# Padding few-row operands and grouping narrow column tiles on TensorE in a two-layer hybrid decoder step

## Chip, cores and metric

The kernel runs on one core of a Trainium2 chip. The metric is the device time of one execution in microseconds (us). The engines are named as the profile names them: PE (TensorE matmuls), PEld (TensorE weight loads), DVE (VectorE), ACT (ScalarE), POOL (GpSimd) and SP (SyncE, which issues most DMAs).

## What is computed

One inference step of a decoder with two layers, on a prompt of 512 tokens and on 8 samples of 4 new tokens each (T = 544 tokens in all, which share every weight). Cut to what matters:

```python
def hybrid_layer(x, conv_hist, S0, mem_k, mem_v, pos, lb, attend, lw):
    hn = rmsnorm(x, norm_g)
    z = hn @ w_in
    (c_h, c_b, c_c, hg_q, hg_f, hg_i, q_lat, kv_lat, k_pe, m_q, sg, mg) = jnp.split(z, offs, axis=-1)
    y_conv = c_b * conv
    o_hg, S = hgrn2_chunked(hg_q * HG_DK ** -0.5, kk, hg_i, logf, S0)
    y_hg = rmsnorm(o_hg, hg_g)
    q = rmsnorm(concat(q_nope, rope(q_pe, pos)), gq)
    c = rmsnorm(kv_lat, kv_norm_g)
    o_lat = attend(q, c, rope(k_pe, pos), w_uk, gk)
    y_mla = o_lat @ w_uv
    y_mem = softmax(rmsnorm(m_q, mem_gq) @ mem_k.T * MEM_SCALE) @ mem_v
    ys = stack([y_conv, y_hg, y_mla, y_mem]) * silu(sg)
    merged = sum(sigmoid(mg) * (ys @ w_bout))
    return x + merged @ w_o, new_hist, S, c, r
```

The prompt attends to itself (MLA) and to a memory of 256 rows. Each sample attends to its own cached latents (2048 past tokens, held in pages), to its own memory keys and values, and has its own HGRN state. All data are float32.

## The kernel before

Activations are held feature-major: 128 features on the partitions, 544 tokens in the columns. The bulk of the work is a list of items (`items`, filled from line 1385 on), each one weight tile of w_in, w_branch_out, w_out or the memory projections. A bulk weight and its operand are each split into a high and a low part of type float32r (`wh`, `wl`; `Hh`, `Hl` and the like), and each product is made of three matmuls of 128 rows, 128 columns and 272 moving columns (half of the tokens), into the PSUM tile `big`. The driver loop loads the next weights (`load`, line 1471), splits them on ACT and DVE (`conv`, line 1478), issues an item's first half, one step of lane A, the second half, the evacuation, and one step of lane B.

The lanes are Python generators that do the rest in plain float32, into the PSUM tile `sm`. A plain float32 matmul stands in the trace as two matmul instructions ("halves" below), a transpose as one.

- Lane A (`lane_a`, line 703): memory attention. For each of 8 samples `s_s` (line 767) makes the scores, four matmuls whose outputs take 32 rows of PSUM each, one per head; `s_t` transposes, `s_v` (line 788) multiplies by the values, eight matmuls of 32 output rows. `load_b` (line 756) loads keys and values of the next sample. Then `hgrn` (line 833), once per head: products inside blocks (`a_mm`), products between blocks of 64 and of 32 tokens, which write 64 and 32 rows of PSUM, the samples' keys and values made token by token in three groups of 32 rows, transposes of values and keys (line 964), and `psy`, eight matmuls of 32 output rows with the samples' states `s0`.
- Lane B (`lane_b`, line 1020): latent attention. `q_mm` (line 1090) multiplies by a weight of 192 rows in two parts, 128 and 64 rows; `k_sum` (line 1074) sums squares of four heads, each into 32 rows; `k_norm` (line 1084) spreads a norm from one row of a group of 32. The samples' softmax over the cached latents is cut into `soft1` to `soft5` (lines 1287 to 1338); `soft2` transposes 16 columns, `soft3` multiplies 16 rows by ones, `soft4` multiplies 17 blocks of probabilities by the latents, the last of them the new tokens (`cnew`, 32 rows).

How many rows an operand has, and how many rows of PSUM its output takes, sets the tiling of the array that a matmul is built with: 128x128, 128x64, 128x32, 64x128, 32x128 or 32x32 (rows x columns). In the built program before, the tiling changes 408 times from one matmul to the next.

The order on each engine is not written by hand. A scheduler with a timeline of its own takes the instructions in the order of the Python code as priorities and moves each to where it expects its operands; on the chip each engine then runs its instructions strictly in that order.

All matmuls go through the helper `mm` (line 169), so that in the trace nearly all are line 170; ACT is line 173, `tensor_tensor` line 179. The lines that the steps below speak of, as they stand:

```python
                mm(ps[64 * hf:64 * hf + 32, 256 + c * 32:256 + (c + 1) * 32], X[32][:, q:q + 32], X[32][:, q + 32:q + 64])
...
            mm(ps[:, 0:16], ones[0:16], g["m"][0:16, 32:48])
...
                mm(ps[:, 0:HT], wuqB[0:64, h * P:(h + 1) * P], qB[0:64, c], start=False)
```

Of the kernel before, what the change touches and what calls it, by code (L numbers as in the profile page):

```python
# [46 lines left out]
def _z_tiles():  # L47
    """Column tiles of w_in: key -> 128 column numbers."""
# [27 lines left out]
# packed gain columns  # L76
# [8 lines left out]
# packed constant columns  # L85
# [51 lines left out]
def hybrid_kernel(ctx: ExitStack, tc: tile.TileContext, a, o):  # L137
# [9 lines left out]
    sp = pool("sp", 10)  # L147
# [21 lines left out]
    def mm(out, lhsT, rhs, start=True, stop=True):  # L169
        TE.matmul(out, lhsT, rhs, start=start, stop=stop)  # L170
# [49 lines left out]
    cnew = kp.tile([TS, P], F32, name="cnew")  # L220
# [11 lines left out]
    row4 = kp.tile([P, P], F32R, name="row4")  # L232
    csq = kp.tile([P, T], F32, name="csq")

    def setup_first():
        V.memset(ones, 1.0)
        V.memset(epsc, EPS)
        x = t("b")[:, 0:P]
        G.memset(x, 0.0)
        for r in range(0, P, 32):  # L240
            G.memset(x[r:r + 1, :], 1.0)
        V.tensor_copy(row4, x)
        S.dma_start(out=gn, in_=a["gains"])

    def scale_rows(s1, s2):
        """The row numbers of the cached latents, by four tokens."""
# [50 lines left out]
    def rstd_small(ss, n, alloc=None, eng=None):  # L297
        """The same for a narrow [rows, w]: a first guess from the exponent, then three Newton steps."""
# [35 lines left out]
    # ------------------------------------------------------------ driver state  # L334
# [17 lines left out]
    # ------------------------------------------------------------ bulk matmuls  # L352
# [60 lines left out]
    # ------------------------------------------------------------ norms of x and memory  # L413
# [55 lines left out]
    def mem_rstd(ms):  # L469
        """1/rms of every memory token, as a column."""  # L470
# [14 lines left out]
    # ------------------------------------------------------------ evacuations  # L485
# [51 lines left out]
    def ev_B(l):  # L537
        def run(it):
            lane[0] = "b"
            qB, rt, tmp = t(), t(), t()  # L540
            act(v2(qB[0:64]), ps2(it)[0:64], AF.Copy)
# [6 lines left out]
            act(sqB[0:64], qB[0:64], AF.Square)  # L548
# [153 lines left out]
    # ------------------------------------------------------------ lane A: memory attention, then HGRN  # L702
    def lane_a(l):
# [52 lines left out]
        def load_b(b):  # L756
            ks, vs = [], []
            for g in range(2):
                k = t()
                SY.dma_start(out=k[:, 0:512], in_=a["mkT"][l, b, :, g * 512:(g + 1) * 512])  # L760
                ks.append(k)
                v = t()
                SY.dma_start(out=v[:, 0:512], in_=a["mv"][l, b, :, g, :])
                vs.append(v)
            kvb[b] = (ks, vs)

        def s_s(b):
            ps = sm()
            for h in range(4):
                mm(ps[32 * h:32 * h + 32, 0:256], mqn[h][:, TP:T], kvb[b][0][h // 2][:, (h % 2) * 256:(h % 2 + 1) * 256])  # L770
# [17 lines left out]
        def s_v(b, pt):  # L788
            ps = sm()
            for j in range(2):  # L790
                for h in range(4):
                    mm(ps[32 * h:32 * h + 32, 0:P], pt[:, 256 + j * P + 32 * h:256 + j * P + 32 * h + 32],
                       kvb[b][1][j][:, h * P:(h + 1) * P], start=(j == 0), stop=(j == 1))
# [5 lines left out]
            del kvb[b]  # L799

        pp, pt_ = {}, {}
        for u in range(6):
            if u == 5:
                load_b(0)
# [28 lines left out]
    def hgrn(l, h):  # L833
# [38 lines left out]
            # one Newton step makes the two exact reciprocals  # L872
# [41 lines left out]
        mm(pss[0:32, 0:32], K4[:, TP:T], Q4[:, TP:T])  # L914
        put(2, ps)
        V.copy_predicated(AT[0:32, TP:T], m8[0:32, 0, 0:32], pss[0:32, 0:32])
# [6 lines left out]
        # factors that leave the chunk  # L923
# [23 lines left out]
        for hf in range(2):  # L947
# [690 lines left out]
```

## Time and profile before

| | |
|---|---|
| median of 3 runs | 1776.54 us (1776.44 to 1778.98) |
| profiled execution, span from first to last instruction | 1777.1 us |
| PE busy | 1751.2 us, 99% of the span, 14058 matmul instructions |
| PEld busy | 1647.5 us, 93% |
| DVE, ACT, POOL busy | 1083.0, 852.2 and 321.7 us (61%, 48%, 18%) |
| DMA | 201.12 MB, mean 113 GB/s |
| TensorE clock granted over the span | 0.997 |

The page gives no other time of the profiled execution than its span. A busy time counts overlapping matmuls once; matmuls are pipelined, so a busy PE may still be losing time between two starts. The page's strip of the span in 40 slices shows PE at nine tenths or more in every slice but the first. The other views used are the timeline (instructions in the order of their starts, equal ones merged), the list of waits, and a table of busy times by stretch.

### The profile page before, as it was taken

Reading aid. Unit: us, or ns where it says so; the run is one execution under the profiler, and the core shown is the slowest. Engines: PE = TensorE matmul, PEld = TensorE weight load, DVE = VectorE, ACT = ScalarE, POOL = GpSimd, SP = SyncE. Lnnn points to the kernel's source line nnn. Section 1 sums busy time; section 2 is a strip of 40 time slices with the busy share of each in tenths; the row PEclk is TensorE's granted clock in tenths of the full one; section 3 lists DMA queues with packets and bytes.
Section 4 is the critical chain, followed back from the end, with each engine's and each line's share of the span. In section 5 each row is a group of like instructions: output and inputs, shape, how many; then the busy total and the mean of one; then the engine's idle time right before and its main releaser. Section 6 shows DMA issues by size and latency. Waiting matters only on the chain.

```text
span 1777.1 us, 36029 instructions
## 1 busy us (share of the span) xinstructions
PE 1751.2 (99%) x14058; PEld 1647.5 (93%) x14058; DVE 1083.0 (61%) x2468; ACT 852.2 (48%) x1651; POOL 321.7 (18%) x327
## 2 busy tenths in 40 slices
PE   7999999999999999999999999999999999999999
PEld 5888889999999999999988798899999999999999
DVE  6666554658787886342464655456788878743332
ACT  5646334655656573222346554355557565622231
POOL 4010001012233432101130100001122343221110
PEclk9999999999999999999999999999999999999999
DMA  6312441233425343223453124423333343232233
GB/s 226 115 60 75 144 144 66 91 119 122 137 87 159 103 149 100 90 78 100 157 166 103 52 95 144 132 65 105 121 123 121 109 143 127 90 105 92 76 115 119
DMA packets 106828, 201.12 MB, mean 113 GB/s; under 512 B 13921, under 2 KB 48098, under 8 KB 106658
## 3 DMA queue, kind: packets, MB, share of 16 engines
q1 hardware_dynamic: 99346, 177.79, 31.5%
q0 software_dynamic: 7168, 20.98, 3.7%
q8 instruction: 111, 1.82, 0.4%
q14 instruction: 59, 0.48, 0.1%
q10 hardware_dynamic: 144, 0.04, 0.0%
HBM read 186.72 MB, written 12.04 MB: 112 GB/s over the span
## 4 chain that ended last, share of the span: by engine, by line
PE 91%; ACT 3%; DVE 3%; issue 2%; POOL 1%; DMA 1%; SPq 0%; ACTq 0%; DVEq 0%
PE big L170 68%; PE sm L170 21%; ACT ta L173 1%; DVE wl L179 1%; ACT wh L173 1%; ACT L173 1%; DVE e L176 1%; PE sm L964 0%; PE sm L739 0%; ACT tb L173 0%; PE sm L1187 0%; DVE Ml L179 0%; PE sm L1268 0%; DMA ta<-in_memT 0%; DVE Hl L179 0%
## 5 line engine op out<-in xcount | busy, mean ns | idle before, releaser
L170 PE MATMUL big<-Hh,wh 128*128 128x272 f32 x2528 | 741.9, 294 | 1.1 <-ACT Hh L173 0.6
L170 PE MATMUL big<-Hh,wl 128*128 128x272 f32 x2528 | 738.4, 292 | 2.8 <-DVE wl L179 2.7
L170 PE MATMUL big<-Hl,wh 128*128 128x272 f32 x2528 | 735.0, 291 | 2.0 <-DVE Hl L179 1.5
L170 PEld LDWEIGHTS big<-Hh,wh 128*128 128x128 f32 x2528 | 477.2, 189 | 12.2 <-issue 7.4
L170 PEld LDWEIGHTS big<-Hh,wl 128*128 128x128 f32 x2528 | 476.2, 188 | 12.1 <-issue 6.3
L170 PEld LDWEIGHTS big<-Hl,wh 128*128 128x128 f32 x2528 | 476.8, 189 | 9.2 <-issue 5.0
L173 ACT ACTIVATE wh<-wr 128x1024 fp32r<-128x1024 f32 (+1 forms) x246 | 232.9, 947 | 465.8 <-PE big L170 384.0
L179 DVE TENSOR_TENSOR wl<-wr,wh 128x1024 fp32r<-128x1024 f32 (+1 forms) x246 | 276.2, 1123 | 262.0 <-ACT wh L173 261.6
L173 ACT ACTIVATE tb<-sm 128x256 f32<-128x256 f32 (+6 forms) x380 | 141.1, 400 | 112.2 <-PE sm L170 84.6
L179 POOL TENSOR_TENSOR M<-M,e 128x544 f32<-128x544 f32 x48 | 87.7, 1827 | 403.5 <-DVE e L176 368.3
L170 PE MATMUL big<-ysh,wl 128*128 128x272 f32 x512 | 149.3, 292 | 0.0
L170 PE MATMUL big<-ysl,wh 128*128 128x272 f32 x512 | 148.4, 290 | 0.0
L170 PE MATMUL big<-ysh,wh 128*128 128x272 f32 x512 | 148.3, 290 | 0.0
L170 PE MATMUL sm<-ta 128*128 128x128 f32 (+5 forms) x1360 | 142.8, 284 | 0.0
L170 PEld LDWEIGHTS sm<-ta 128*128 128x128 f32 (+2 forms) x1360 | 106.6, 148 | 21.3 <-issue 9.6
L173 ACT ACTIVATE ta<-ta 128x544 f32<-128x544 f32 (+3 forms) x180 | 95.5, 538 | 52.4 <-DVE ta L179 38.9
L179 DVE TENSOR_TENSOR ta<-ta 128x256 f32<-128x256 f32 (+3 forms) x248 | 111.1, 481 | 10.1 <-ACT ta L173 9.3
L170 PE MATMUL sm<-Rh,rb 128*128 128x272 f32 x512 | 105.0, 294 | 0.0
L1206 POOL DMA_INDIRECT tb<-in_lat,row4i x64 | 72.0, 1125 | 180.2 <-PE sm L170 65.9
L1206 POOL DMA_INDIRECT tb<-in_rop,row4i x64 | 73.0, 1141 | 171.6 <-PE sm L170 56.2
L188 DVE TENSOR_REDUCE s<-tb 128x8 f32<-128x512 f32 (+1 forms) x150 | 99.8, 671 | 5.1 <-issue 4.6
L170 PEld LDWEIGHTS big<-ysh,wh 128*128 128x128 f32 x512 | 96.4, 188 | 0.7 <-issue 0.4
(233 smaller groups left out, 2551.2 us busy)
## 6 DMA issues: line engine op xcount, KB each, us to landing
wr<-in_w_in SPq DMA_DIRECT2D x158, 512.0 KB
wr<-in_wb SPq DMA_DIRECT2D x64, 256.0 KB
tb<-in_latT SPq DMA_DIRECT2D x256, 64.0 KB
ta<-in_mkT SPq DMA_DIRECT2D x32, 256.0 KB
ta<-in_mv SPq DMA_DIRECT2D x32, 256.0 KB
wr<-in_wo SPq DMA_DIRECT2D x16, 512.0 KB
ta<-in_shg SPq DMA_DIRECT2D x16, 256.0 KB
out_hgs<-ta SPq DMA_DIRECT2D x16, 256.0 KB
```

Source lines behind the costliest of these rows:

```text
L170: TE.matmul(out, lhsT, rhs, start=start, stop=stop)
L173: S.activation(out, in_, f, **k)
L176: V.scalar_tensor_tensor(out=out, in0=in0, scalar=sc, in1=in1, op0=op0, op1=op1)
L179: (eng or V).tensor_tensor(out=out, in0=in0, in1=in1, op=op)
L188: V.tensor_reduce(out=out, in_=in_, op=op, axis=AX.X, **k)
L1206: G.indirect_dma_start(out=out, out_offset=None, in_=a[src], in_offset=bass.IndirectOffsetOnAxis(ap=idx, axis=0))
```

## The change

Operands of few rows get the full 128 rows, with zeros below (`qB`, `wuqB`, `wukT` to 96 rows, `cnew`, `row4`, the small softmax tile `m`, the samples' HGRN products), so that their matmuls have the tiling 128x128 or stay in the one around them. Products of narrow outputs that stood apart are put together: `issue_after(first)` queues what is traced in its block behind the matmul `first` on PE. The HGRN products between blocks of 64 tokens are made in two halves of 32 rows. The samples' keys and values in HGRN are copied four times side by side by POOL and transposed as full tiles, where six matmuls made them. Memory keys are loaded two samples ahead and values two steps ahead of their use. In the built program the tiling changes 118 times. Zeros are written by POOL. The count of weight tiles and of bulk matmuls stays.

```diff
-    sp = pool("sp", 10)
+    sp = pool("sp", 8)
+    mp = pool("mp", 2)
...
-    row4 = kp.tile([P, P], F32R, name="row4")
+    row4 = kp.tile([P, 4, P], F32R, name="row4")
...
+            G.memset(qB[64:128], 0.0)
...
         for u in range(10):
+            first = s_v(u - 2, ss.pop(u - 2)) if u >= 2 else None
             if u < 8:
-                ss[u] = s_s(u)
+                with (tc.issue_after(first.ins) if first else nullcontext()):
+                    ss[u] = s_s(u)
             if 1 <= u < 9:
                 ss[u - 1] = s_t(ss[u - 1])
-            if u >= 2:
-                s_v(u - 2, ss.pop(u - 2))
-            if u + 1 < 8:
-                load_b(u + 1)
+            load_b(u + 2, "k")
+            load_b(u, "v")
...
-        mm(pss[0:32, 0:32], K4[:, TP:T], Q4[:, TP:T])
+        mm(pss[:, 0:TS], K4[:, T - P:T], Q4[:, TP:T])
...
-        ps = sm()
+        ps, psy = sm(), sm()
+        first = None
         for c in range(4):
             o_ = c * P
-            mm(ps[0:64, c * 64:(c + 1) * 64], X[64][:, o_:o_ + 64], X[64][:, o_ + 64:o_ + P])
-            for hf in range(2):
-                q = o_ + 64 * hf
-                mm(ps[64 * hf:64 * hf + 32, 256 + c * 32:256 + (c + 1) * 32], X[32][:, q:q + 32], X[32][:, q + 32:q + 64])
+            for r in (0, 32):
+                i = mm(ps[r:r + 32, c * 64:(c + 1) * 64], X[64][:, o_ + r:o_ + r + 32], X[64][:, o_ + 64:o_ + P])
+                first = first or i
+        with tc.issue_after(first.ins):
+            for c in range(4):
+                for r in (0, 64):
+                    q = c * P + r
+                    mm(ps[r:r + 32, 256 + c * 32:256 + (c + 1) * 32], X[32][:, q:q + 32], X[32][:, q + 32:q + 64])
+            for b in range(NB):
+                j, g = b % 4, b // 4
+                mm(psy[32 * j:32 * j + 32, g * P:(g + 1) * P], qe[:, TP:T], s0[g][:, j * P:(j + 1) * P])
...
+        rp = t()
+        for x, c in ((vv, 0), (ke, P)):
+            G.tensor_copy(rp[:, c:c + P].rearrange("p (r q) -> p r q", r=4), bcl(x[:, TP:T], 4))
         ps = sm()
-        for x, c in ((vv, 0), (ke, P)):
-            for r in range(0, 96, 32):
-                mm(ps[r:r + 32, c:c + P], x[:, TP:T], ident)
+        for c in (0, P):
+            TE.transpose(ps[:, c:c + P], rp[:, c:c + P], ident)
...
-        mm(pso[:, 0:32], sk[0:32, 0:P], AT[0:32, TP:T], stop=False)
+        mm(pso[:, 0:32], sk[:, 0:P], AT[:, TP:T], stop=False)
...
-            mm(srcs[hf][:, 0:HT], ones[0:64], sqB[0:64, c], start=False)
+            mm(srcs[hf][:, 0:HT], ones, sqB[:, c], start=False)
...
-            for h in range(4):
-                mm(ps[32 * h:32 * h + 32, :], ones[0:96, 0:32], sqk.pop(h)[0:96, 0:TP])
+            first = mm(ps[96:128, :], ones[0:96, 0:32], sqk.pop(3)[0:96, 0:TP])
+            with tc.issue_after(first.ins):
+                for h in range(3):
+                    mm(ps[32 * h:32 * h + 32, :], ones[0:96, 0:32], sqk.pop(h)[0:96, 0:TP])
...
-                mm(ps, row4[32 * h:32 * h + 32, :], x[32 * h:32 * h + 32, 0:TP], start=(n == 0), stop=(n == 1))
+                mm(ps, row4[:, h, :], x[:, 0:TP], start=(n == 0), stop=(n == 1))
...
-                mm(ps[:, 0:HT], wuqB[0:64, h * P:(h + 1) * P], qB[0:64, c], start=False)
+                mm(ps[:, 0:HT], wuqB[:, h * P:(h + 1) * P], qB[:, c], start=False)
...
-            mm(ps[:, h * 32:(h + 1) * 32], wukT[0:64, h * P:(h + 1) * P], Q[0:64, h, TP:T])
+            mm(ps[:, h * 32:(h + 1) * 32], wukT[0:96, h * P:(h + 1) * P], Q[0:96, h, TP:T])
...
-            x = g["m"] = s_()
+            x = g["m"] = mp.tile([P, P], F32, tag="m", name="m")
+            G.memset(x, 0.0)
...
-            TE.transpose(ps[0:16, 0:P], g["m"][:, 0:16], ident)
+            TE.transpose(ps[:, 0:P], g["m"], ident)
...
-            mm(ps[:, 0:16], ones[0:16], g["m"][0:16, 32:48])
+            mm(ps[:, 0:16], ones, g["m"][:, 32:48])
...
-                    mm(ps[0:32, 0:P], two[0:32], cnew, start=False)
+                    mm(ps[0:32, 0:P], two, cnew, start=False)
```

How the order moves is shown at three places. A row is an instruction with its line, its output and operands, and the output's rows x columns; "x4" counts equal rows that follow each other. The changed kernel has one line more ahead of `mm`, so its matmuls are line 171.

PE, the second head's products between blocks in `hgrn` (`ta` are lane A's tiles, `tb` lane B's, `cst` the identity), before and then in the change; they follow a `soft4`:

```order
L170 MATMUL sm<-tb,S 32x128 x16
L170 MATMUL sm<-cnew,S 32x128
L170 MATMUL sm<-ta 64x64
L170 MATMUL sm<-ta 32x32 x2
...
L170 MATMUL sm<-cst,ta 32x128 x6
L964 MATMUL sm<-cst,ta 128x128 x4
L170 MATMUL big<-Hl,wh 128x272
```

```order
L171 MATMUL sm<-tb,S 32x128 x16
L171 MATMUL sm<-cnew,S 32x128
L171 MATMUL sm<-ta 32x64 x8
L171 MATMUL sm<-ta 32x32 x8
L171 MATMUL sm<-ta 32x128 x8
L971 MATMUL sm<-cst,ta 128x128 x2
L171 MATMUL big<-Hh,wh 128x272
```

Four pairs of one 64-row and two 32-row products alternated; they now stand sorted, all 32 rows high, with the eight `psy` products behind them (32x128 x8), and two transposes take the place of six products. Before, `psy` stood alone between bulk matmuls 14 of them later.

PE, the scores of the memory attention's samples (`s_s`, outputs 32x256; `s_v`'s are 32x128), before and then in the change:

```order
L170 MATMUL sm<-ta 32x256 x2
L170 MATMUL big<-Hl,wh 128x272
L170 MATMUL big<-Hh,wl 128x272
L784 MATMUL sm<-cst,ta 128x128 x2
L170 MATMUL sm<-ta 32x128 x8
...
L170 MATMUL sm<-ta 32x256 x2
```

```order
L171 MATMUL sm<-ta 32x128 x8
L171 MATMUL big<-Hh,wh 128x272
L171 MATMUL big<-Hl,wh 128x272
...
L171 MATMUL sm<-ta 32x256 x4
L785 MATMUL sm<-cst,ta 128x128 x2
```

Fourteen of the 16 `s_s` (8 samples, 2 layers) were cut into two pairs, one per loaded key tile, with other work between; in the change all 16 are whole, and four of them follow an `s_v` directly.

POOL, around the second head's copies for the two transposes (line 968), in the change; before, the copies were not there and the rest stood in the same order:

```order
L180 TENSOR_TENSOR ra<-ra,cst 96x512 x2
L1333 MEMSET S 128x16
L1222 DMA tb<-in_rop,row4i 128x128 x4
L1222 DMA tb<-in_lat,row4i 128x512 x2
L914 MEMSET ta 128x544
...
L1222 DMA tb<-in_lat,row4i 128x512 x2
L1222 DMA tb<-in_rop,row4i 128x128 x4
L968 COPY ta<-ta 128x128 x2
```

The two copies, on which the transposes L971 wait, stand behind the gathers of lane B (line 1222) in POOL's queue.

## Rows read from the trace of the kernel before

**Rows 1.** The page: busy time of PE, and the chain that ended last, by engine.
```profile
PE 1751.2 (99%) x14058; PEld 1647.5 (93%) x14058; DVE 1083.0 (61%) x2468; ACT 852.2 (48%) x1651; POOL 321.7 (18%) x327
...
PE 91%; ACT 3%; DVE 3%; issue 2%; POOL 1%; DMA 1%; SPq 0%; ACTq 0%; DVEq 0%
```

**Rows 2.** Timeline of PE: start us, us, what; eleven bulk starts, first and last.
```profile
601.09 0.29 PE L170 MATMUL big<-Hh,wh 128*128 128x272 f32 x1
...
602.34 0.29 PE L170 MATMUL big<-Hl,wh 128*128 128x272 f32 x1
```

**Rows 3.** Timeline of PE: eight plain halves at 128x128 between bulk matmuls.
```profile
372.87 0.28 PE L170 MATMUL big<-Hh,wh 128*128 128x272 f32 x1
372.99 1.00 PE L170 MATMUL sm<-QR,tb 128*128 128x64 f32 x8
...
374.01 0.29 PE L170 MATMUL big<-Hh,wl 128*128 128x272 f32 x1
```

**Rows 4.** Timeline of PE: `psy`, sixteen halves in four column groups, alone.
```profile
436.57 0.29 PE L170 MATMUL big<-Hh,wl 128*128 128x272 f32 x1
436.79 0.64 PE L170 MATMUL sm<-ta 128*32 128x128 f32 x16
...
437.59 0.29 PE L170 MATMUL big<-Hl,wh 128*128 128x272 f32 x1
```

**Rows 5.** Timeline of PE: one of the 28 half `s_s`.
```profile
209.91 0.29 PE L170 MATMUL big<-Hh,wl 128*128 128x272 f32 x1
210.13 0.62 PE L170 MATMUL sm<-ta 128*32 128x256 f32 x4
...
210.92 0.29 PE L170 MATMUL big<-Hl,wh 128*128 128x272 f32 x1
```

**Rows 6.** Timeline of PE: `cnew`, then HGRN's products between blocks, to the transposes.
```profile
431.46 0.40 PE L170 MATMUL sm<-cnew,S 32*32 32x128 f32 x2
431.79 1.81 PE L170 MATMUL sm<-ta 128*64 128x64 f32 x22
...
434.00 0.66 PE L964 MATMUL sm<-cst,ta 128*128 128x128 f32 x4
```

**Rows 7.** Timeline of PE: one of the 8 matmuls of `k_sum`.
```profile
145.29 0.29 PE L170 MATMUL big<-Hh,wh 128*128 128x272 f32 x1
145.51 1.05 PE L170 MATMUL sm<-tb,ones 96*32 96x512 f32 x2
...
146.72 0.29 PE L170 MATMUL big<-Hh,wl 128*128 128x272 f32 x1
```

**Rows 8.** Timeline of PE: one head of `q_mm`, parts of 128 and 64 rows in turn.
```profile
93.90 0.29 PE L170 MATMUL big<-Hh,wl 128*128 128x272 f32 x1
94.02 2.58 PE L170 MATMUL sm<-tb 128*128 128x272 f32 x8
...
96.76 0.29 PE L170 MATMUL big<-Hl,wh 128*128 128x272 f32 x1
```

**Rows 9.** Timeline of PE: `soft3`, 16 rows, one of 16.
```profile
421.14 0.29 PE L170 MATMUL big<-Hl,wh 128*128 128x272 f32 x1
421.35 0.39 PE L170 MATMUL sm<-s,ones 16*128 16x16 f32 x2
...
421.90 0.30 PE L170 MATMUL big<-Hh,wh 128*128 128x272 f32 x1
```

**Rows 10.** Timeline of PE: `soft2`, the transpose of 16 columns, one of 16.
```profile
403.31 0.28 PE L170 MATMUL big<-Hl,wh 128*128 128x272 f32 x1
403.43 0.27 PE L1306 MATMUL sm<-cst,s 128*16 128x128 f32 x1
...
403.66 0.29 PE L170 MATMUL big<-Hh,wh 128*128 128x272 f32 x1
```

**Rows 11.** Busy time by stretch: stretch, length, PE, PEld, DVE, ACT, POOL (instructions), granted clock, DMA.
```profile
330.00:620.00 290.00, 289.02 (x2523) 279.46 (x2522) 223.55 (x549) 170.47 (x359) 79.64 (x72) 1.00 0.38 119
```

**Rows 12.** Waits, all engines: who, for whom, us in total, times, longest us.
```profile
POOL tb L1206 <- PE sm L170: 122.1, 17, 21.7
```

More of the change, by code (lines that the diff above doesn't have):

```diff
@@ L1 @@
-from contextlib import ExitStack, contextmanager
+from contextlib import ExitStack, contextmanager, nullcontext
 import numpy as np
@@ L169, in mm @@
     def mm(out, lhsT, rhs, start=True, stop=True):
-        TE.matmul(out, lhsT, rhs, start=start, stop=stop)
+        return TE.matmul(out, lhsT, rhs, start=start, stop=stop)
     def act(out, in_, f, **k):
@@ L219, in hybrid_kernel @@
     ctokP = kp.tile([P, 4, P], F32, name="ctokP")
-    cnew = kp.tile([TS, P], F32, name="cnew")
+    cnew = kp.tile([P, P], F32, name="cnew")
     x1 = dp.tile([P, KD, T], F32, name="x1")
@@ L237, in setup_first @@
         V.memset(epsc, EPS)
-        x = t("b")[:, 0:P]
+        x = t("b")[:, 0:4 * P].rearrange("p (h q) -> p h q", h=4)
         G.memset(x, 0.0)
-        for r in range(0, P, 32):
-            G.memset(x[r:r + 1, :], 1.0)
+        for h in range(4):
+            G.memset(x[32 * h:32 * h + 1, h, :], 1.0)
         V.tensor_copy(row4, x)
+        G.memset(cnew, 0.0)
         S.dma_start(out=gn, in_=a["gains"])
@@ L547, in run @@
             sqB = t()
-            act(sqB[0:64], qB[0:64], AF.Square)
+            act(sqB, qB, AF.Square)
             st[l].update(qB=qB, rt=rt, r2=r2, sqB=sqB)
@@ L754, in lane_a, with load_b @@
         kvb = {}
[L756 to L765, printed above, removed]
+        def load_b(b, which):
+            if b < NB:
+                for g in range(2):
+                    x = t()
+                    src = a["mkT"][l, b, :, g * 512:(g + 1) * 512] if which == "k" else a["mv"][l, b, :, g, :]
+                    SY.dma_start(out=x[:, 0:512], in_=src)
+                    kvb.setdefault((which, b), []).append(x)
         def s_s(b):
@@ L798, in s_v @@
                 tt(st[l]["acc"][:, 0:P], ps[:, 0:P], st[l]["acc"][:, 0:P], ALU.add)
-            del kvb[b]
+            del kvb["v", b]
+            return first
         pp, pt_ = {}, {}
@@ L938, in hgrn @@
         yield
-        ps = sm()
+        ps, psy = sm(), sm()
+        first = None
         for c in range(4):
             o_ = c * P
-            mm(ps[0:64, c * 64:(c + 1) * 64], X[64][:, o_:o_ + 64], X[64][:, o_ + 64:o_ + P])
-            for hf in range(2):
-                q = o_ + 64 * hf
-                mm(ps[64 * hf:64 * hf + 32, 256 + c * 32:256 + (c + 1) * 32], X[32][:, q:q + 32], X[32][:, q + 32:q + 64])
+            for r in (0, 32):
+                i = mm(ps[r:r + 32, c * 64:(c + 1) * 64], X[64][:, o_ + r:o_ + r + 32], X[64][:, o_ + 64:o_ + P])
+                first = first or i
+        with tc.issue_after(first.ins):
[6 more added lines that the diff above has]
+                mm(psy[32 * j:32 * j + 32, g * P:(g + 1) * P], qe[:, TP:T], s0[g][:, j * P:(j + 1) * P])
         act(at3[0:64, :, 64:P], ps[0:64, 0:256].rearrange("p (c q) -> p c q", c=4), AF.Copy)
-        for hf in range(2):
-            r = slice(64 * hf, 64 * hf + 32)
-            act(at3[r, :, 64 * hf + 32:64 * hf + 64], ps[r, 256:384].rearrange("p (c q) -> p c q", c=4), AF.Copy)
+        for r in (0, 64):
+            act(at3[r:r + 32, :, r + 32:r + 64], ps[r:r + 32, 256:384].rearrange("p (c q) -> p c q", c=4), AF.Copy)
         vt, kt, sk = t(), t(), t()
+        rp = t()
+        for x, c in ((vv, 0), (ke, P)):
+            G.tensor_copy(rp[:, c:c + P].rearrange("p (r q) -> p r q", r=4), bcl(x[:, TP:T], 4))
         ps = sm()
-        for x, c in ((vv, 0), (ke, P)):
-            for r in range(0, 96, 32):
-                mm(ps[r:r + 32, c:c + P], x[:, TP:T], ident)
-        act(sk[0:32, 0:P], ps[0:32, 0:P], AF.Copy)
+        for c in (0, P):
+            TE.transpose(ps[:, c:c + P], rp[:, c:c + P], ident)
+        act(sk[:, 0:P], ps[:, 0:P], AF.Copy)
         s3 = tr()
         act(s3[0:96, 0:256], ps[0:96, 0:256], AF.Copy)
+        act(sk[:, 256:512], psy[:, 0:256], AF.Copy)
         for r, c in ((32, 0), (64, P)):
@@ L971, in hgrn @@
             vb.append(x)
-        psy = sm()
-        for b in range(NB):
-            j, g = b % 4, b // 4
-            mm(psy[32 * j:32 * j + 32, g * P:(g + 1) * P], qe[:, TP:T], s0[g][:, j * P:(j + 1) * P])
-        act(sk[:, 256:512], psy[:, 0:256], AF.Copy)
         yield
@@ L1051, in lane_b @@
         TE.transpose(ps[0:32, 0:P], cT[:, TP:T], ident)
-        act(cnew, ps[0:32, 0:P], AF.Copy)
+        act(cnew[0:32, :], ps[0:32, 0:P], AF.Copy)
         for i in range(2):
@@ L1119, in lane_b @@
         wukT = t()
+        G.memset(wukT[64:96, 0:512], 0.0)
         SY.dma_start(out=wukT[0:64, 0:512], in_=a["wukT"][l])
```

13 lines of the change are left out of this document (8 added, 5 removed).

## Prediction

> **What bounds the kernel now.** Read the page first: PE is busy 1751.2 of 1777.1 us, and the chain that ended last is 91% PE [rows 1]. No other engine is near; so the time is the sum of what PE does, plus the little that it waits. A busy PE hides lost time, though, because matmuls overlap: the price of a matmul is the distance from its start to the next start, and that is read from the timeline. The reader is to see three prices there.
>
> A bulk matmul: ten distances take 602.34 - 601.09 = 1.25 us, 0.125 us each [rows 2].
>
> A plain half in the full array: from the last bulk start ahead of it to the second bulk start behind it 1.14 us pass; less two bulk distances, 0.89 us for eight halves, 0.111 us each [rows 3]. They have 64 columns, so at or below 128 columns I take 0.11 us whatever the width; a plain product of two halves costs 0.22 us, a transpose 0.11 us.
>
> A change of tiling: sixteen halves of `psy`, in four column groups, cost 1.02 - 0.25 = 0.77 us by the same reckoning [rows 4]. Sixteen in a row would be 1.8 us; four column groups side by side make four passes of 0.11 us, and 0.32 us is left over for leaving 128x128 and coming back. Half an `s_s` has only two column groups, two passes of 256 columns, and costs 1.01 - 0.25 = 0.76 us [rows 5]: the same 0.32 us and 0.22 us a pass. So an excursion costs 0.32 us whatever it holds, and filling it up to four column groups costs nothing. That is what the change buys.
>
> The bulk work, its order and its count stay, so I price the sites where the tiling changes, against the profiled execution's 1777.1 us (its runs' median is 0.6 us lower, and 0.2% of the time, 3.6 us, is about what a measurement can tell from no change).
>
> **The change part by part.**
>
> Memory scores: before, 28 half `s_s` at 0.76 us and two whole ones, taken at 0.77 us: 22.8 us. After, 12 whole ones alone at 0.76 us (four column groups in the same two passes) and four behind an `s_v`, which pay their passes alone, 0.44 us: 10.9 us. Gain 11.9 us. What it needs is both key tiles at once; keys are loaded two samples ahead for it, on an SP queue with the same number of loads. `s_s` is queued behind an `s_v` that is two samples older, so it waits longer than before, with no tight reader: its own `s_v` comes two steps later.
>
> HGRN: from the first 64-row product to the transposes 434.00 - 431.79 = 2.21 us pass, and `psy` costs 0.77 us later: 2.98 us a head [rows 6, 4]. After, 48 halves stand in one excursion that exists before too. In rows 4 a pass of four column groups is 0.11 us, 0.028 us a half; by that 48 halves are 1.33 us. The 64-token and 32-token products use two column groups only, a row of which the trace does not show by itself; if each of their 16 passes cost a full 0.11 us, it would be 2.2 us. I take 1.33 us, since their halves move 64 and 32 columns and not 128. Two transposes add 0.22 us. Gain 1.43 us a head, 11.4 us for eight; in the first head of each layer the six-product group was split once more by a change (0.32 us), so 12.0 us, or 4.3 us at the other end. The copies that POOL makes for the transposes are new (16, one instruction each); I cost them at nothing, since they are ready to be made as soon as `ke` is, and POOL is busy 79.64 of 290 us there [rows 11]. That cover is a rival below.
>
> Key sums: eight matmuls, each alone, 1.43 - 0.25 = 1.18 us, 9.4 us [rows 7]. After, four in one excursion, twice, again 1.18 us each: gain 7.1 us. Queueing three of them behind the last-made one costs nothing, since all four must be there before anything goes on.
>
> Latent queries: eight halves of 272 columns, 128 and 64 rows in turn, cost 2.86 - 0.25 = 2.61 us [rows 8]. At 0.22 us per 256 columns a half of 272 costs 0.23 us, eight 1.84 us, so the two excursions cost 0.77 us. This pattern stands six times in `q_mm` and twice at `sqB`; two more heads have one excursion: 8 x 0.77 + 2 x 0.39 = 7.0 us. The zeros are written by POOL before the weights and `qB` arrive; if POOL were late there, one wait per layer would come of it, not one per head.
>
> `soft3`: 0.76 - 0.25 = 0.51 us before, 0.22 us after [rows 9]: 16 x 0.29 = 4.6 us. The product of `sk` has the same form, 8 x 0.29 = 2.3 us. The zeroing of `m` goes to POOL ahead of a reduction on DVE; two buffers of `m` make it ready one sample early.
>
> `cnew` in `soft4`: 431.79 - 431.46 = 0.33 us [rows 6], after at most two halves, 0.22 us: 16 x 0.11 = 1.8 us, between 0 and 0.2 us each, 3.2 us.
>
> Small ones. `K4` by `Q4`: an excursion of two narrow halves (0.32 + 0.06 us) becomes 0.22 us, 8 x 0.16 = 1.3 us. `wukT`: two excursions go, 0.6 us. The new keys' products lose 0.6 us, since the order cuts them into two excursions per layer where there was one. `row4`: 16 products of 512 columns, padded, cost about 0.125 x 512 / 272 = 0.24 us each, 3.8 us; six excursions go, 1.9 us, but products in different row groups may have run side by side before. I take nothing, between a loss of 0.9 us (four at once before: 1.0 + 1.9 us against 3.8 us) and a gain of 1.9 us.
>
> `soft2`, by contrast, changes nothing: its transpose had a narrow tiling, yet costs 0.35 - 0.25 = 0.10 us [rows 10], what a full one does. So of the 290 changes that go, these 32 were free. The Trainium skill says otherwise, in "TensorEngine Tiling (Array Packing)", Key Properties: any change of tiling mode drains TensorE. By that rule alone these 16 excursions would give back another 16 x 0.32 = 5.1 us, 1724 us; the row shows nothing to give back, so the sum stays.
>
> Sum: 11.9 + 12.0 + 7.1 + 7.0 + 4.6 + 2.3 + 1.8 + 1.3 + 0.6 - 0.6 + 0 = 48.0 us. 1777.1 - 48.0 = **1729 us**. With all low ends (HGRN -7.7, `row4` -0.9, `cnew` -1.8) 1740 us, with the high ones (`row4` +1.9, `cnew` +1.4) 1726 us.
>
> **The rivals.**
>
> *Padding gives up work side by side.* If the 32-row products overlapped before, the padded ones cost more. For it: four column groups do overlap [rows 4]. Against it: `soft3` and the 64-row parts have no partner in another row group and took 0.51 and 2.61 us as they were [rows 8, 9]; only `row4` has partners. It would give 1729 + 0.9 = 1730 us; 10%, inside the forecast's range. This is the rule of the Trainium skill that speaks against the change: "TensorE: Matmul & The Clock Gate", Part 3, says that small matmuls in different row groups run concurrently and should be sliced so; no row here shows row groups doing it.
>
> *The lanes become the bound.* Between 330 and 620 us DVE is busy 223.55 of 290 us [rows 11], and PE would be some 11 us shorter there. If the HGRN, softmax and small terms of this stretch and its twin in layer 2, 12.0 + 4.6 + 2.3 + 1.8 + 1.3 = 22 us, came back as waits on DVE and ACT, the time is 1751 us. Against it: PE is busy 289.02 of the 290 us now, and DVE's share would only go from 77% to 80%. 7%.
>
> *The price lies in the narrow form, not in the change.* Then whole `s_s` and `k_sum` cost what their parts did, and about 19 us of the sum are not there: 1748 us. Against it: four halves and sixteen cost the same [rows 4, 5]. 3%.
>
> *Slower: POOL holds PE.* In HGRN the two transposes now wait for copies that stand behind lane B's gathers in POOL's queue, and all bulk work stands behind the transposes in PE's. The gathers wait for PE 17 times, 122.1 us, 7.2 us on average [rows 12]. If a copy were late by that in all eight heads, 57 us come on top: 1786 us. It decides from 48 / 8 = 6 us a head. Against it: what the gathers wait for stands earlier on PE, and in the fourth head of a layer no gather stands right ahead of the copies. 3%; a late copy or two lie inside the range.
>
> **How the numbers follow.** The forecast, with the first rival, has 87%, its own range 1724 to 1740 us. The range of 8 in 10 goes a little beyond it on both sides, 1720 to 1746 us, for waits that the new order brings or takes. Slower by over 0.2% is the POOL case, 3%; within 0.2% I give 2%, where two rivals meet; faster 95%.
>
> **What would show it.** Step by step: whole `s_s` of eight halves in 0.76 us between bulk matmuls; one chain of 16 + 16 + 16 halves in HGRN within 1.6 us to the transposes' end; `k_sum` in two excursions of 1.2 us; eight halves of `q_mm` in 1.85 us; `soft3` in 0.22 us; bulk distances of 0.125 us as before; and PE's idle time unchanged. It is wrong if PE shows idle time ended by POOL at the transposes of line 971, if bulk distances grew, or if the two-column-group passes cost a full 0.11 us each.

## The result, and the profile after

The changed kernel takes 1735.53 us (median of 4 runs, 1734.46 to 1735.84) against 1776.55 us: a ratio of 0.9764, 95% interval [0.9751, 0.9778], 41.0 us less. Forecast were 1729 us, from 48.0 us less. The direction and most of the size are right; some 7 us of the gain are missing.

Two things about the times have to be known: in some executions PE waits 2.0 to 2.4 us at the start for POOL, in others not, so that times fall into two groups some 2.5 us apart (before: 1775.9 to 1776.9 and 1778.8 to 1779.4 us; the profiled execution of before had that wait, the one of after had not), and one of the six executions of the control further down took 4475.92 us and is not counted.

The page of after, to be read against [rows 1]:

```profile
span 1733.2 us, 36030 instructions
...
PE 1704.0 (98%) x14042; PEld 1642.6 (95%) x14042; DVE 1079.2 (62%) x2468; ACT 849.7 (49%) x1651; POOL 333.2 (19%) x366
...
PE 86%; DVE 6%; ACT 4%; issue 2%; DMA 1%; SPq 1%; POOL 0%; ACTq 0%; DVEq 0%
```

PE's busy time fell by 1751.2 - 1704.0 = 47.2 us, which is nearly the whole sum of the forecast. But the chain that ended last has less PE in it (86%, was 91%) and more DVE, and PE's idle time did not stay: it was 1777.1 - 1751.2 = 25.9 us, of which 2.1 us are the wait at the start; it is 1733.2 - 1704.0 = 29.2 us. Without the start that is 5.4 us more. So 47.2 - 5.4 = 41.8 us were left, and the question is where 5.4 us of new waits stand. The list of PE's waits, of after and then of before (who, for whom, us in total, times, longest):

```profile
PE big L171 <- DVE wl L180: 3.9, 8, 0.8
PE sm L171 <- ACT wh L174: 2.8, 2, 1.4
...
PE sm L171 <- DVE S L1276: 2.0, 2, 1.7
...
PE sm L971 <- DVE S L1276: 1.6, 2, 0.8
```

```profile
PE big L170 <- DVE wl L179: 4.0, 9, 0.8
PE sm L170 <- POOL sl L179: 2.1, 1, 2.1
...
PE sm L170 <- issue: 1.3, 2, 0.6
```

The reader is to see three groups that are new: `sm <- ACT wh`, twice 1.4 us (before twice 0.65 us, under "issue"); `sm <- DVE S`, 2.0 us in two pieces, one of them 1.7 us; and the transposes of line 971, twice 0.8 us. That is 1.5 + 2.0 + 1.6 = 5.1 us.

The prices themselves came out as the forecast had them. Timeline of PE after: a whole `s_s` of four column groups, one head of `q_mm`, and `soft3`, to be read against [rows 5, 8, 9].

```profile
177.78 0.28 PE L171 MATMUL big<-Hh,wl 128*128 128x272 f32 x1
177.99 0.64 PE L171 MATMUL sm<-ta 128*32 128x256 f32 x8
...
178.79 0.29 PE L171 MATMUL big<-Hl,wh 128*128 128x272 f32 x1
...
91.41 0.29 PE L171 MATMUL big<-Hh,wl 128*128 128x272 f32 x1
91.53 2.00 PE L171 MATMUL sm<-tb 128*128 128x272 f32 x8
...
93.49 0.29 PE L171 MATMUL big<-Hl,wh 128*128 128x272 f32 x1
...
403.61 0.29 PE L171 MATMUL big<-Hl,wh 128*128 128x272 f32 x1
403.74 0.29 PE L171 MATMUL sm<-m,ones 128*128 128x16 f32 x2
...
404.08 0.29 PE L171 MATMUL big<-Hh,wh 128*128 128x272 f32 x1
```

By the reckoning of the forecast (from the bulk start ahead to the second bulk start behind, less 0.25 us) these are 1.01 - 0.25 = 0.76 us for eight halves, where before four halves cost as much; 2.08 - 0.25 = 1.83 us for `q_mm`; and 0.47 - 0.25 = 0.22 us for `soft3`. The HGRN chain of the third head:

```profile
501.52 0.29 PE L171 MATMUL big<-ysl,wh 128*128 128x272 f32 x1
501.64 0.29 PE L171 MATMUL sm<-m,ones 128*128 128x16 f32 x2
501.86 1.08 PE L171 MATMUL sm<-tb,S 128*32 128x128 f32 x32
...
502.98 1.30 PE L171 MATMUL sm<-ta 128*32 128x64 f32 x46
504.21 0.44 PE L971 MATMUL sm<-cst,ta 128*128 128x128 f32 x2
...
504.61 0.29 PE L171 MATMUL big<-ysh,wh 128*128 128x272 f32 x1
```

All of it costs 504.61 - 501.52 - 0.25 = 2.84 us. The same `soft3` and `soft4` without a chain behind them cost 539.68 - 537.90 - 0.25 = 1.53 us in the same trace:

```profile
537.90 0.29 PE L171 MATMUL big<-Hh,wl 128*128 128x272 f32 x1
...
539.68 0.29 PE L171 MATMUL big<-Hl,wh 128*128 128x272 f32 x1
```

So 48 halves and two transposes are 1.31 us. Forecast were 1.33 + 0.22 = 1.55 us.

### The profile page after: what moved, and what is told of

Same layout as the page of the kernel before. It is cut to its first block, busy times and chain, and to the rows that moved or that the text cites. A ratio compares the mean times of both kernels' runs of the same rounds, so it can differ in the third digit from the quotient of the medians.

```text
span 1733.2 us, 36030 instructions
## 1 busy us (share of the span) xinstructions
PE 1704.0 (98%) x14042; PEld 1642.6 (95%) x14042; DVE 1079.2 (62%) x2468; ACT 849.7 (49%) x1651; POOL 333.2 (19%) x366
## 4 chain that ended last, share of the span: by engine, by line
PE 86%; DVE 6%; ACT 4%; issue 2%; DMA 1%; SPq 1%; POOL 0%; ACTq 0%; DVEq 0%
PE big L171 66%; PE sm L171 18%; DVE ta L180 1%; DVE wl L180 1%; DMA tb<-in_latT 1%; ACT ta L174 1%; ACT tb L174 1%; ACT wh L174 1%; DVE e L177 1%; ACT L174 1%; SPq L1244 0%; PE sm L1203 0%; PE sm L981 0%; DVE Ml L180 0%; DMA ta<-in_memT 0%
## 5 line engine op out<-in xcount | busy, mean ns | idle before, releaser
L180 POOL TENSOR_TENSOR M<-M,e 128x544 f32<-128x544 f32 x48 | 96.9, 2019 | 358.4 <-DVE e L177 349.2
L171 PE MATMUL sm<-ta 128*128 128x128 f32 (+6 forms) x1424 | 122.5, 279 | 0.3
L171 PEld LDWEIGHTS sm<-ta 128*32 128x32 f32 (+1 forms) x1424 | 101.2, 147 | 9.0 <-issue 2.8
```

Source lines behind the costliest of these rows:

```text
L171: return TE.matmul(out, lhsT, rhs, start=start, stop=stop)
L180: (eng or V).tensor_tensor(out=out, in0=in0, in1=in1, op=op)
```

## Experiments

### The four parts, each alone on the kernel before

They tell whether the terms of the sum hold one by one, and in which part the missing gain stands. First the memory scores (the diff of the part is in the section on the change: `load_b`, `s_s` queued behind `s_v`):

> The kernel before with one part of the change alone: the memory scores made whole, keys loaded two samples ahead, scores queued behind the values' products. Theory (an excursion out of 128x128 and back costs 0.32 us whatever it holds): 28 half and 2 whole scores become 16 whole ones, 12 alone and 4 behind another narrow group, 11.9 us less than before. Rival (the price lies in the narrow form itself): the same 64 narrow matmuls cost the same, 0 us. Rival (keys or PSUM late): the order brings waits at the scores, and less than 8 us comes back.

The HGRN part (from `ps, psy = sm(), sm()` to the padded product of `sk`, with `K4` by `Q4`):

> The kernel before with the HGRN part alone: products between blocks 32 rows high, sorted, with the states' products behind them, samples' keys and values copied by POOL and transposed as full tiles, the samples' product inside blocks padded. Theory: 12.0 + 2.3 + 1.3 = 15.6 us less, less what the fourth head of each layer waits at the two transposes (0.9 us twice in the changed kernel). Rival (POOL's copies late behind the gathers): a wait at the transposes ended by POOL, some us per head, and less than 10 us of gain. Rival (two-column-group passes at a full 0.11 us each): 15.6 - 7.7 = 7.9 us less.

The key sums (`first = mm(...)` and `issue_after` in `k_sum`, nothing else):

> The kernel before with the four key sums queued together alone. In the built program the eight excursions of the key sums become two, but the scheduler then cuts the row products of the key norms into eight excursions where there were six. Theory: 7.1 us less for the sums, 0.6 us more for the two other excursions, 6.5 us less in all. Rival (narrow form): 0 us. Rival (any change of tiling costs by itself, 0.16 us each): only 4 of 408 changes go in sum, so 0.6 us less.

The padded operands (`cnew`, `row4`, `qB`, `sqB`, `wuqB`, `wukT`, `m`):

> The kernel before with the zero-padded operands alone (latent queries' second part, its squares, the row products of the key norms, the new latents, the latent-key weights, the small softmax tile), HGRN and memory attention as before. Theory: 7.0 + 4.6 + 1.8 + 0.6 = 14.0 us less, with between -0.9 and +1.9 us more of gain from the row products. Rival (side-by-side work in row groups is lost): less than 13 us. Rival (every change of tiling costs, transposes of 16 columns too): 5.1 us more gain, 19 us.

Measured: the medians with their intervals, the group of runs without the wait at the start (before: 1776.5 us), and, from the traces, the time from the 276th bulk matmul to the last, in which the start has no part (before 1772.97 - 74.06 = 1698.91 us).

| part | median, ratio | without the wait at the start | 276th to last bulk matmul | forecast |
|---|---|---|---|---|
| memory scores | 1764.92 us, [0.9916, 0.9949] | 1764.8: -11.7 | 1687.19: -11.7 | -11.9 |
| HGRN | 1761.55 us, [0.9892, 0.9925] | 1761.4: -15.1 | 1684.34: -14.6 | -15.6 |
| key sums | 1775.00 us, [0.9975, 0.9994] | 1772.8: -3.7 | 1695.04: -3.9 | -6.5 |
| padding | 1770.77 us, [0.9944, 0.9973] | 1769.5: -7.0 | 1691.83: -7.1 | -14.0 |
| all, the change | 1735.53 us, [0.9751, 0.9778] | 1735.5: -41.0 | 1657.04: -41.9 | -48.0 |

What follows: the two large parts give what was forecast, and the rival of a price that lies in the narrow form (0 us for the scores) falls. HGRN alone keeps its gain with POOL's copies in it, so "POOL holds PE" falls too. The key sums give 3.7 us for four changes of tiling less, so 0.16 us for each change alone (0.6 us) does not describe them; but most of their gain is four sums that share their time, and whether the count of changes is the price is settled only by the kernels further down. Padding gives half. Its page has PE busy for 1738.0 us of 1770.3 us: the busy time fell by 13.2 us, as forecast (14.0), and the idle time rose by 6.4 us. The gain is made, and half of it is then waited away.

The key sums lose in another way. The eight excursions became two of 1.2 us each, but the scheduler then laid the row products of `k_norm` differently. Timeline of PE: before, four of them together; then the same four in the run with the key sums alone; then in the run with the padding alone (each trace has its own times).

```profile
169.81 0.73 PE L170 MATMUL sm<-rb,row 32*128 32x512 f32 x4
```

```profile
167.49 0.73 PE L170 MATMUL sm<-rb,row 32*128 32x512 f32 x2
...
168.85 0.72 PE L170 MATMUL sm<-rb,row 32*128 32x512 f32 x2
```

```profile
166.89 1.17 PE L171 MATMUL sm<-rb,row 128*128 128x512 f32 x4
```

Four products of two heads, which lie in two different groups of 32 rows, take 0.73 us, and two products of one head, in one group of rows, take the same 0.73 us. So row groups do run side by side here. Cut into two excursions, the four cost that twice: the second one, which is new, adds 0.85 us in each layer by the reckoning above. The products of the new keys also stand in two excursions per layer where there was one, 1.74 us and not 1.43 us. That is 2.3 us, of which 0.6 us had been expected; PE's idle time rose by another 0.9 us without the start (24.7 us, and 25.9 - 2.1 = 23.8 us before). Together these are the missing 2.6 us. In the change itself the row products' part of it isn't there, because they are padded too.

### Does every change of tiling cost, or only some?

Two kernels, each with one thing of the change undone; both have 150 changes of tiling where the change has 118, and apart from that the same order of instructions.

```diff
-            TE.transpose(ps[:, 0:P], g["m"], ident)
+            TE.transpose(ps[0:16, 0:P], g["m"][:, 0:16], ident)
```

> The changed kernel with one thing undone: the small softmax transpose takes 16 columns again, so that it is built with 32 columns of the array. 16 places, 32 changes of tiling more (150 instead of 118), nothing else moves. Theory (this kind of change was free before): 0 us against the changed kernel, 1735.5 us. Rival (every change of tiling costs 0.16 us): 32 x 0.16 = 5.1 us more, 1740.6 us.

```diff
-            mm(ps[:, 0:16], ones, g["m"][:, 32:48])
+            mm(ps[:, 0:16], ones[0:32], g["m"][0:32, 32:48])
```

> The changed kernel with one other thing undone: the ones product of the small softmax has 32 rows again instead of 128. Again 16 places, 32 changes of tiling more (150 instead of 118), and nothing else moves: the same count as in the run with the 16-column transposes. Theory: 16 x (0.51 - 0.22) = 4.6 us more than the changed kernel, 1740.1 us. Rival (the count of changes as such costs nothing, the narrow outputs of other places did): 0 us.

Measured: 1737.97 us (1737.5 to 1738.42) and 1741.49 us (1740.68 to 1743.04). Timeline of PE, one site of each: a transpose with 16 columns, and a `soft3` with 32 rows.

```profile
385.70 0.28 PE L171 MATMUL big<-Hl,wh 128*128 128x272 f32 x1
385.83 0.27 PE L1323 MATMUL sm<-cst,m 128*16 128x128 f32 x1
...
386.06 0.29 PE L171 MATMUL big<-Hh,wh 128*128 128x272 f32 x1
```

```profile
403.49 0.28 PE L171 MATMUL big<-Hl,wh 128*128 128x272 f32 x1
403.70 0.39 PE L171 MATMUL sm<-m,ones 32*128 32x16 f32 x2
...
404.25 0.29 PE L171 MATMUL big<-Hh,wh 128*128 128x272 f32 x1
```

The transpose costs 0.36 - 0.25 = 0.11 us, what the full one costs; all 16 sites agree with the changed kernel to 0.01 us. The `soft3` of 32 rows costs 0.76 - 0.25 = 0.51 us against 0.22 us. Over its 16 sites the `soft3` adds between 0.16 and 0.30 us each, 4.0 us in all (least where it stands beside other products). Equal counts of changes, 32 each, and one adds nothing at its sites while the other adds 4.0 us: the count is not the price. By the Trainium skill, "TensorEngine Tiling (Array Packing)", Key Properties, both should have drained TensorE; the rows show a cost for the products and none for these transposes.

The total of the first run is 2.4 us above the changed kernel all the same. In its trace this time lies at five places where PE waits, the largest at a product with the latents (1.5 us at 1521 us), none at a transpose. The run with the 32-row `soft3` and the one of the next section, which has no narrow transposes and 118 changes, are of the same series and have the two largest of them at the same places; the control below, of a later series, has neither. So they go with the series rather than with the edit, but that series had no control, and what caused them stays open.

### What do the transposes of line 971 wait for?

```diff
-                mm(psy[32 * j:32 * j + 32, g * P:(g + 1) * P], qe[:, TP:T], ...)
+                mm(psy[32 * j:32 * j + 32, 256 + g * P:256 + (g + 1) * P], qe[:, TP:T], ...)
...
-        ps = sm()
+        ps = psy
         for c in (0, P):
             TE.transpose(ps[:, c:c + P], rp[:, c:c + P], ident)
```

> The changed kernel with the states' products of HGRN and the two transposes of the samples' keys and values in one PSUM tile and not in two. Theory (the wait at the transposes in each layer's fourth head, 0.8 us in the list of waits and ended by DVE, is one for a PSUM tile, since the change holds two at a time there): both waits go, 1.6 us less than the changed kernel, 1733.9 us. Rival (the transposes wait for POOL's copies): the waits stay, 1735.5 us.

Measured: 1738.39 us (1736.77 to 1740.66), no gain. What the engine of line 971 sat idle for just before it (what ended it: us, times), in the changed kernel and then in this one:

```profile
  issue: 3.3, 8
  DVE S L1276: 1.6, 2
```

```profile
  issue: 1.6, 8
```

The wait is gone with the second PSUM tile, and POOL's copies are as they were. So it was a wait for a PSUM tile: in the change `ps`, `psy` and the transposes' tile are held at once, of four, while lane B's products with the latents hold the others until DVE has copied them. But the time did not come back: in this kernel the next transposes (line 981) wait 0.9 us for the same DVE line, and the waits `sm <- DVE S` are four. The cause is shown; that the 1.6 us can be had is not.

### A later lane B

PE waits 1.4 us in each layer ahead of the first `q_mm`. Timeline: PE before, PE after, and ACT before and after, where it reads the sums that the norm of the latent queries comes from.

```profile
86.77 0.29 PE L170 MATMUL big<-Hh,wh 128*128 128x272 f32 x1
87.70 1.15 PE L170 MATMUL sm<-tb 128*128 128x272 f32 x4 [0.65 <-issue]
```

```profile
83.92 0.29 PE L171 MATMUL big<-Hh,wh 128*128 128x272 f32 x1
85.62 1.16 PE L171 MATMUL sm<-tb 128*128 128x272 f32 x4 [1.42 <-ACT wh L174]
```

```profile
79.76 0.86 ACT L173 ACTIVATE tb<-sm,epsc 128x272 f32<-128x272 f32 x2
```

```profile
77.68 0.86 ACT L174 ACTIVATE tb<-sm,epsc 128x272 f32<-128x272 f32 x2
```

ACT is 2.08 us earlier and so is the first `q_mm`: that is the wait at the start, which this execution did not have. The bulk matmul ahead of `q_mm` is 2.85 us earlier. The 0.77 us between them is what the padding of `sqB` had gained just ahead, and it ends as a wait for ACT's and DVE's norm, in each layer. Can it be had by taking lane B one step of the driver later?

```diff
+        yield
         for h in range(4):
             q_mm(h)
             yield
```

> The changed kernel with lane B one step of the driver later from the first latent queries on. Theory (PE waits 1.4 us in each layer at the first latent queries, because the scheduler's timeline places them ahead of the end of the norm on ACT and DVE): both waits go, 2.8 us less, against one excursion more per layer in the built order (122 changes), 0.6 us: 2.2 us less than the changed kernel, 1733.3 us. Rival (waits move to the next reader or to the end of lane B): 1735.5 us or more.

Measured: 1770.09 us (1765.85 to 1771.89), ratio to before [0.9938, 0.9973]: 34.6 us slower than the change. The page, and two stretches of 2 us (stretch, length, PE, PEld, DVE, ACT, POOL, granted clock, DMA):

```profile
PE 1721.0 (97%) x14042; PEld 1649.3 (93%) x14042; DVE 1079.4 (61%) x2468; ACT 851.8 (48%) x1651; POOL 327.5 (19%) x366
...
428.00:430.00 2.00, 0.43 (x5) 0.27 (x6) 0.00 (x0) 0.00 (x0) 1.04 (x2) 1.00 0.12 33
...
432.00:434.00 2.00, 2.00 (x11) 2.00 (x11) 0.62 (x3) 1.87 (x4) 1.39 (x2) 0.53 0.00 0
```

The two waits are gone from the list, as the theory had it. But PE's idle time is 1769.5 - 1721.0 = 48.5 us, 19.3 us more than in the change (2.0 us of it the wait at the start), and its busy time is 17.0 us more. The longest new waits are 2.9 us in each layer, at a bulk matmul that waits for DVE. Another 6.3 us in 15 pieces stand mostly in the HGRN chains, which no longer stand behind a `soft4`: the chain at 426 us cost 5.6 us, where one alone costs 1.95 us in the change. What the chains waited for the trace doesn't name ("issue"); that stays open. After PE had been busy 0.43 of the 2 us from 428 to 430 us, the granted clock of the next two such stretches was 0.61 and 0.53, nearly the lower of its two levels (1.2 of 2.4 GHz), and bulk distances were 0.225 us. Over the whole span the granted clock is 0.993, in the change 0.997, so that the clock can account for some 7 us of the loss (an estimate, 0.4% of 1769.5 us). The edit moved the built order of both lanes in both layers; so this run shows that lane B's step is worth more than the wait in front of it, and not what each part of the loss comes from.

### Transfers that are no longer hidden

The longest new wait, 1.7 us, in the timeline of the changed kernel (PE, then ACT):

```profile
640.32 0.29 PE L171 MATMUL big<-Hh,wl 128*128 128x272 f32 x1
642.32 0.52 PE L171 MATMUL sm<-Rh,rb 128*128 128x272 f32 x2 [1.72 <-DVE S L1276]
```

```profile
640.83 0.63 ACT L174 ACTIVATE rb<-tb 128x512 fp32r<-128x512 f32 x1 [4.09 <-DMA tb<-in_latT]
```

ACT splits the transposed latents when their transfer lands, then reads the PSUM tiles that PE waits for; the split stands ahead of that in ACT's queue. The test loads them one unit earlier, beside a control, the changed kernel unaltered:

```diff
-        for k in range(2):
+        for k in range(3):
             get_t(*units[k])
...
-            nb, nq = ahead(n, 2)
+            nb, nq = ahead(n, 3)
```

> The changed kernel once more, unaltered, for comparison with the other runs. Theory (some of PE's waits in it are for transfers of the latents and differ from one series of runs to the next; the run with the 16-column transposes showed 3.0 us more of them at five places, with the 16 transposes themselves unchanged): up to 3 us more than the 1735.5 us of its first runs, between 1735.5 and 1738.5 us, and the difference lies at the first products with the latents after bulk matmuls. Rival (the extra time of that run was the price of its 32 changes): 1735.5 us again.

> The changed kernel with the transposed latents loaded three units ahead of their use and not two. Theory (PE now reaches the products with the latents before their transfer has landed; 1.7 us at 640 us of the changed kernel, and some tenths at 464 and 1320 us): these waits go, 2 to 3 us less than the changed kernel run beside it. Rival (the transfers stand behind weight loads in SP's queue, whose start is set by a free weight buffer, or the extra tile in flight makes other readers wait): no gain, or some us more.

Measured: control 1735.14 us (median of five, 1734.58 to 1738.33); its runs without the wait at the start 1734.58 to 1735.14 us. So the changed kernel repeats, and the extra time that the theory allowed for isn't there; the rival's reason for the run with the narrow transposes, a price of its changes, was ruled out at the sites above. Earlier loads: 1732.46 us (1731.49 to 1734.38), 0.9744 [0.9730, 0.9758] of before. Between the 276th and the last bulk matmul the traces have 1657.29 us for the control and 1654.09 us for this run, 3.2 us less, and the place itself has no wait any more:

```profile
642.26 0.29 PE L171 MATMUL big<-Hh,wh 128*128 128x272 f32 x1
642.38 0.41 PE L171 MATMUL sm<-Rh,rb 128*128 128x272 f32 x2
```

Set against each other bulk matmul by bulk matmul, the two traces differ by 1.7 us at this place and by 0.4 us at another product with the latents (1322 us in the control). Another 1.0 us, half of it in each layer, lies where PE waits for a split weight (479 and 1335 us in the control); there the built order is another, too, so this part is not shown to be the transfer's. The transfer's part of the shortfall, some 2 us, can be had.

That a faster PE caught up with the transfer is not what the traces show. Timeline of SP, the eight loads to which this transfer belongs, before and then in the change:

```profile
647.23 5.80 SPq L1228 DMA_DIRECT2D tb<-in_latT  x8
```

```profile
634.99 4.96 SPq L1244 DMA_DIRECT2D tb<-in_latT  x8
```

Before, they stand behind the 77th weight load in SP's queue, and the product that waits in the change starts 659.42 - 647.23 = 12.2 us after the first of them. In the change they stand behind the 79th, and that product starts 642.32 - 634.99 = 7.3 us after the first, with 1.7 us of wait in it. With the earlier load this transfer stands behind the 77th again and starts at 620.6 us. So the new built order had moved the transfer back in SP's queue, and the earlier load undoes it. The wait at line 971 is still in this run (1.6 us), and so is the one at `q_mm` (2.8 us).

### The new keys in one excursion

```diff
-        mm(ps[0:32, 0:256], cT[:, TP:T], wuk[:, 0:256])
...
+        first = mm(ps1[0:32, 0:P], rt[64:96, TP:T], qrs[64:96, 0:P], start=False)
+        with tc.issue_after(first.ins):
+            mm(ps[0:32, 0:256], cT[:, TP:T], wuk[:, 0:256])
```

> The changed kernel with the new keys' product queued behind the two products with the samples' queries, so that they stand in one excursion per layer and not in two (56 excursions in all, 58 before). Theory: 0.5 us per layer less (1.94 us in two excursions, 1.43 us in one), 1.0 us less than the changed kernel run beside it, if no wait takes its place. Rival (the small norm of the new keys, which now starts later, is late for the samples' scores): no gain.

Measured: 1734.94 us (1734.47 to 1737.86); without the wait at the start 1734.5 to 1735.0 us, as the control. Timeline of PE: the bulk matmuls around the control's two excursions, and around the one of this run.

```profile
175.55 0.28 PE L171 MATMUL big<-Hh,wl 128*128 128x272 f32 x1
...
177.67 0.29 PE L171 MATMUL big<-Hh,wl 128*128 128x272 f32 x1
```

```profile
173.29 0.29 PE L171 MATMUL big<-Hh,wl 128*128 128x272 f32 x1
...
175.08 0.29 PE L171 MATMUL big<-Hl,wh 128*128 128x272 f32 x1
```

Less the bulk distances inside (three and two), the two excursions cost 2.12 - 0.375 = 1.74 us and the one costs 1.79 - 0.25 = 1.54 us, in both layers: 0.2 us less, not 0.5. The 1.94 us of the expectation add up two stretches that overlap. The order differs from before, too: there the products of the new keys come first, the tiling changes once inside the excursion, and it costs 1.43 us; here it changes three times inside. The tiling changes 118 times in both traces, with one excursion per layer less in this one; so here, too, the count of changes is not the price. The rest of what the trace gains (1656.22 us between the bulk matmuls named above, 1.1 us less than the control's) are waits elsewhere, and the runs don't show it. Both edits together:

> The changed kernel with both edits that gained: the transposed latents loaded three units ahead and the new keys' product queued behind the samples' queries. Theory: the two gains add, 3.2 us from the transfers (1731.5 us against 1734.9 us in the runs without the wait at the start) and up to 1.0 us from two excursions less: 1730.5 to 1731.7 us in the runs without the wait at the start, some 2.5 us more in those with it. Rival (the later norm of the new keys is late now that the rest is faster): 1732 us or more in the runs without that wait.

Measured: 1732.29 us (1731.38 to 1733.99), 0.9751 [0.9738, 0.9765] of before, no better than the earlier loads alone. Those are the step to keep; at some 1732.4 us it beats both kernels.

## Why the prediction was right, and where it was off

- **An excursion costs 0.32 us whatever it holds: right** where one tiling holds inside it. It carries the whole sum, and the sites bear it out: 0.76 us for a whole `s_s` as for half of one, 0.22 us for a `soft3` that stays in 128x128 and 0.51 us for one that doesn't. Changes inside an excursion add to it: the same products of the new keys cost 1.43 us with one of them and 1.54 us with three.
- **The terms: right in sum.** PE's busy time fell by 47.2 us, forecast were 48.0. HGRN gave more (1.31 us and not 1.55 us a head, 1.9 us in all: a half that moves 64 or 32 columns in two column groups is no dearer than one in four). The new keys lost 0.6 us, as forecast (1.74 us a layer and not 1.43). Two sums of the prediction are slightly off without moving its centre: the low end of HGRN is 5.0 us by its own numbers (12.0 us less 8 times 2.2 - 1.33 us) and not 4.3, and the latent queries' terms make 6.9 us and not 7.0.
- **"PE's idle time unchanged": wrong**, and this is the step that failed. It rose by 5.4 us without the start: 1.5 us ahead of the first `q_mm`, where the gain of `sqB` met ACT's norm; 2.0 us at two products with the latents, the larger one for a transfer that the new order issues behind two more weight loads; 1.6 us at line 971 for a PSUM tile. The forecast let every place at which PE gets faster count in full and asked only for POOL's copies what would be late next; of SP's queue it looked at the number of loads, which stayed, and not at their order, which did not. Its high end of 1746 us was set "for waits that the new order brings", its centre was not.
- **The base.** From the span of 1777.1 us were taken 48.0 us to get a time. The span is that of an execution with the wait at the start, and 2.2 us lie around it (1735.38 us of time for a span of 1733.2 us after). The two nearly cancel, so that the base was 0.6 us above the median by luck.
- **Row groups side by side**, at 10%, was the mechanism that runs: two heads' row products share their time (0.73 us for four as for two). "No row here shows" it was a misreading: the merged rows of the timeline hide starts 3 ns apart, and only a comparison of groups of different size shows it. As the Trainium skill says in "TensorE: Matmul & The Clock Gate", Part 3, such products overlap; the padding gives that up, and what it gains in excursions makes up for it, so that the 0 us taken for `row4` held.
- **The lanes become the bound**, at 7%: not as priced (22 us), but the 5.4 us are of its kind, waits on ACT, DVE and a transfer.
- **POOL holds PE**: no wait at line 971 was ended by POOL.

## What to carry to other kernels

Price a change of tiling at the site, from the start ahead to the second start behind: an excursion has one price, so fill it, with one tiling inside, or pad the operand and stay. When PE is the bound, sum the gain of each place only up to the next point at which PE needs something from a chain that does not get faster (a norm on ACT, a PSUM tile), and take the rest as a wait; look, too, where the new order puts each transfer in its queue. Here these waits were a ninth of the sum. Loading one unit earlier brought the transfer's part back.

## What the hardware showed that was not expected

- A transpose that uses 16 columns of the array costs what a full one costs (0.11 us), although it is built with a change of tiling on either side; a product of 32 rows pays 0.29 us for such changes.
- Two heads' products of 32 rows and 512 columns in different row groups take no longer than one head's (0.73 us).
- A transfer that the new order put behind two more weight loads in SP's queue made PE wait 1.7 us, though the number of loads was the same.
- One step more of delay in a lane cost 34.6 us: 19.3 us more of idle time, and 17.0 us more of busy time, of which the lower granted clock explains some 7 us.
